# The value rows of a PEER expert layer, loaded by indirect transfers from GpSimd's queue instead of plain transfers from the SP queue

## The chip, the cores and the metric

The kernel runs on one core of one Trainium2 chip. Its engines are TensorE (PE for the multiplications, PEld for the weight loads that overlap them), VectorE (DVE), ScalarE (ACT), GpSimd (POOL) and SyncE (SP). Transfers between DRAM and the on-chip buffers are issued from the queue of an engine and carried out by the core's 16 DMA engines. The metric is device time in microseconds (us), lower is better.

## What is computed

One decoder layer on 256 tokens of width 1024: modulated norms, an input projection, two kinds of attention, their gated merge, and then a PEER feed-forward layer, in float32. Only the end of that last layer is touched by the change:

```python
def peer_ffn(h, w_pq, peer_keys, peer_u, peer_v):
    ...                      # routing: 128 experts of 16384 and a gate for each, per token
    u = jnp.take(peer_u, ec, axis=0)
    act = jax.nn.gelu(jnp.einsum('cd,ckd->ck', xc, u))
    vv = jnp.take(peer_v, ec, axis=0)
    return jnp.einsum('ck,ckd->cd', gc * act, vv)
```

`peer_v` has 16384 rows of 1024 floats, 64 MB in all. The kernel does not gather a token's 128 experts: it works out the activations of all 16384 experts for all tokens, multiplies them with gates that are zero for every expert that a token did not choose, and multiplies the result with the whole of `peer_v`. So every row of `peer_v` is read once, in an order that is known when the kernel is built.

## The kernel before, in words

The experts form a grid of 128 by 128. Expert number i * 128 + j stands in row i and column j, and the kernel takes one column j at a time: the 128 experts of a column lie on the 128 partitions. Two neighbouring columns make a pair, so there are 64 pairs.

The U side (`upair`, L551) works out the activations of a pair: 48 matmuls of 256 columns into `pus` or `pum`, then a gelu. For the first 58 pairs (columns below `J0` = 116) this is done early, beside the routing, and the result, 256 KB per pair, goes to DRAM (`act_spill`). The other 6 pairs, called direct here, are worked out in the V stage itself.

The V stage (from L740) is where the change lies. `order` (L747 to L752) mixes the 6 direct pairs with the 58 stored ones: two direct pairs first, then a direct one after each 12 or so stored ones. The loop at L778 takes the pairs in that order. For each pair it

- loads the stored activations `a` of the pair two places ahead from the SP queue (`act_of`, L758), into one of two buffers,
- multiplies `a` with the gates in place (`weighted`, L764, on DVE) and splits the product into a rounded part `wh` (ACT, L81) and the rest `wl` (DVE, L82); the end of `wl` frees the `a` buffer,
- loads the value rows of its two columns (`unit`, L784, which issues L91), 512 KB for each column: partition i gets row i * 128 + j, 4 KB, so the 128 rows of one load lie 512 KB apart in DRAM; each is split into `h_v` (ACT, L81) and `l_v` (DVE, L82), and the end of `l_v` frees the load's buffer `raw`,
- issues 24 matmuls of 512 columns into `acc` (`v_mm`, L85 to L87 through `mm3`).

The load's buffer has the tag `raw` and four places, which the U side's loads (`r_u`) and the V side's (`r_v`) share and take in turn; `hi` and `lo` have four places each as well. `a`, `wh` and `wl` have two. The order of the instructions on each engine is set when the kernel is built, by a scheduler that goes by priorities and modelled times; an engine then works through its list in order, and an instruction that waits holds up what is behind it on the same engine. GpSimd has no work in the kernel before but four small memsets at its start.

Before the V stage, the gate grid is built (`grid_mm`, L709, matmuls `pg` at L714) from buffers of the pool `onehot`, which are closed at L737, and their room is given to the pools of the V stage, `weights_in` and `weighted` (L741, L742). After it come the residual and the last norm.

Of the kernel before, what the change touches and what calls it, by code (L numbers as in the profile page):

```python
# [7 lines left out]
F32 = mybir.dt.float32  # L8
# [10 lines left out]
P = 128  # L19
# [4 lines left out]
EPS = 1e-6  # L24
# activations of the first J0 columns of experts are worked out while the routing goes on and kept in DRAM
J0 = 116
# steps of the routing, and batches of gates, to a pair of such columns
PACE_R = 2.5
PACE_G = 2.0
# the first norm's scales (even) and shifts (odd) that the tensor engine works out  # L30
ON_PE = (0, 1, 2, 3)
# [3 lines left out]
def kernel(  # L35
# [25 lines left out]

# [1 line left out]
    cpool = ctx.enter_context(tc.tile_pool(name="consts", bufs=1))  # L63
# [32 lines left out]
    def rsqrt(r, m, q, n=1):  # L96
        # 1 / sqrt(m) for n columns, halves m: first guess from the exponent, then Newton steps to float32's
        # accuracy
        nc.vector.tensor_scalar(r.bitcast(I32), m.bitcast(I32), 1, None, op0=OP.arith_shift_right)
        nc.vector.tensor_scalar(  # L100
            r.bitcast(I32), r.bitcast(I32), -1, 0x5F3759DF, op0=OP.mult, op1=OP.add
        )
        nc.vector.tensor_scalar(m, m, -0.5, None, op0=OP.mult)
        for _ in range(3):
            for i in range(n):
                c = slice(i, i + 1)
                nc.vector.scalar_tensor_tensor(q[:, c], r[:, c], r[:, c], m[:, c], op0=OP.mult, op1=OP.mult)
            for i in range(n):
                c = slice(i, i + 1)
                nc.vector.scalar_tensor_tensor(r[:, c], q[:, c], 1.5, r[:, c], op0=OP.add, op1=OP.mult)  # L110
# [10 lines left out]

# [1 line left out]
    es_a = ExitStack()  # L123
# [38 lines left out]
    def ada1(k):  # L162
        # scale and shift of row block k; some from the weights as they come on the tensor engine
        raw = spool.tile([P, 2, D], F32, tag="ada", bufs=3, name=f"ada1_{k}")
        nc.sync.dma_start(raw, w_ada[2 * k : 2 * k + 2].rearrange("k p d -> p k d"))
        got = []
        for i in range(2):
            t = 2 * k + i
            if t in ON_PE:
                row = pp.tile([1, P], F32, tag="pp", name=f"row_{t}")  # L170
                wk = raw[:, i].rearrange("p (k n) -> p k n", k=NC8)
                for j in range(NC8):
                    nc.tensor.matmul(row, cc[:, j : j + 1], wk[:, j], start=(j == 0), stop=(j == NC8 - 1))
                rs = spool.tile([1, P], F32, tag="rs", bufs=2, name=f"rs_{t}")
                nc.scalar.activation(rs, row, AF.Copy, scale=-1.0)
                cm = pm.tile([P, 1], F32, tag="mm", name=f"cm_{t}")
                nc.tensor.matmul(cm, rs, neg_one[0:1, 0:1], start=True, stop=True)
                got.append(cm)
            else:
                dots(raw[:, i : i + 1], t)  # L180
                got.append(mod[:, t : t + 1])
        g, b = gs[:, 0, k : k + 1], mod[:, 2 * k + 1 : 2 * k + 2]
        nc.vector.scalar_tensor_tensor(
            g, got[0], bcol1[:, k : k + 1], gcol[:, 0, k : k + 1], op0=OP.add, op1=OP.mult
        )
        nc.vector.tensor_add(b, got[1], bcol[:, 2 * k + 1 : 2 * k + 2])
        return g, b
# [10 lines left out]
    def rms(sq, name):  # L198
        # 1 / rms with tokens on partitions, then along them on all partitions
        ms = pz.tile([P, 2], F32, tag="z", name=f"ms_{name}")  # L200
        for tt in range(2):
            for i, s in enumerate(sq):
                nc.tensor.matmul(
                    ms[:, tt : tt + 1], s[:, P * tt : P * tt + P], mean_m,
                    start=(i == 0), stop=(i == len(sq) - 1),
                )
        rq = spool.tile([P, 3, 2], F32, name=f"rq_{name}")
        nc.vector.tensor_scalar(rq[:, 0], ms, EPS, None, op0=OP.add)
        rsqrt(rq[:, 1], rq[:, 0], rq[:, 2], 2)
        r = pm.tile([P, T], F32, tag="mm", name=f"r_{name}")  # L210
        for tt in range(2):
            dg = spool.tile([P, P], F32, tag="sq", bufs=2, name=f"dr_{name}{tt}")
            nc.vector.tensor_scalar(dg, ident, rq[:, 1, tt : tt + 1], -1.0, op0=OP.mult, op1=OP.mult)
            nc.tensor.matmul(r[:, P * tt : P * tt + P], neg_one, dg, start=True, stop=True)
        return r
# [19 lines left out]
    for k in range(NC8):  # L235
        nc.vector.tensor_mul(xr[:, k], x_sb[:, k], r1)
    # the first column blocks, for q and k, take each row block of h as its modulation arrives
    hh, hl = h_tiles("n1")
# [42 lines left out]

# [1 line left out]
    q_sb = apool.tile([P, 4, T], F32, name="q_sb")  # L283
# [26 lines left out]
    def roped(dst, ps, name):  # L310
        t1 = spool.tile([P, 2, T], F32, tag="att", bufs=6, name=f"t1_{name}")
        t2 = spool.tile([P, 2, T], F32, tag="att", bufs=6, name=f"t2_{name}")
        nc.vector.tensor_mul(t1, ps, rp[:, 0:1].to_broadcast([P, 2, T]))
        nc.vector.tensor_mul(t2, ps, rp[:, 1:2].to_broadcast([P, 2, T]))
        # rows of a pair of tiles: heads 0 2 1 3; two heads of 64 rows to each tile that is kept
        for i in range(2):
            nc.vector.tensor_sub(dst[:, i], t1[:, 0], t2[:, 1])
        for i, to, at in ((0, 32, 0), (0, 96, 64), (1, 0, 32), (1, 64, 96)):
            nc.vector.tensor_add(dst[to : to + 32, i], t2[at : at + 32, 0], t1[at : at + 32, 1])
# [23 lines left out]

# [1 line left out]
    o_hi = apool.tile([P, 6, T], F32R, name="o_hi")  # L345
# [48 lines left out]

# [1 line left out]
    def dilated(h, o):  # L396
# [81 lines left out]

# [1 line left out]
    m_hi = hpool.tile([P, NC8, T], F32R, tag="hh", name="m_hi")  # L480
# [65 lines left out]

# [1 line left out]
    es_s = ExitStack()  # L548
# [23 lines left out]

# [1 line left out]
    sel_pool = es_s.enter_context(tc.tile_pool(name="sel", bufs=1, side="right"))  # L574
    # per slot (head, rank): both halves of its expert's number, its gate in three parts
    selT = sel_pool.tile([P, 5, T], BF16, name="selT")
# [15 lines left out]
    for b in range(1, 8):  # L592
# [4 lines left out]
        nc.scalar.activation(qT[:, 2 * b : 2 * b + 2], ps, AF.Copy)  # L597
    # x1 with tokens on partitions, for the end
    for tt in range(2):
# [20 lines left out]
    for tt in range(2):  # L620
# [16 lines left out]
        nc.vector.tensor_copy(i_top, i_u)  # L637
        # pairs (a, b) of ranks with (a + 1) * (b + 1) > 16 have 16 pairs before them, so
        # a < 4 with every b and a >= 4 with b < 4 hold the 16 best, in the order of a * 16 + b
        cand = rpool.tile([P, 8, 112], F32, tag="cand", name=f"cand{tt}")  # L640
# [61 lines left out]

# [1 line left out]
    gpool = ctx.enter_context(tc.tile_pool(name="grid", bufs=1))  # L704
# [4 lines left out]
    def grid_mm(b, A, Bs):  # L709
        # a gate's parts add up to it without error  # L710
        ps = pg.tile([P, 4, P], F32, tag="g", name=f"pg{b}")
# [27 lines left out]

# [1 line left out]
    apl = ctx.enter_context(tc.tile_pool(name="weights_in", bufs=2))  # L741
    wpool = ctx.enter_context(tc.tile_pool(name="weighted", bufs=2))  # L742
    po = ctx.enter_context(tc.tile_pool(name="po", bufs=1, space=PSUM))
    acc = [po.tile([P, 512], F32, name=f"acc{i}") for i in range(4)]
    vv = v.rearrange("(i j) d -> j i d", j=NJ)
    direct, stored = list(range(J0, NJ, 2)), list(range(0, J0, 2))
    order = [direct.pop(0)]  # L747
    while direct or stored:
# [29 lines left out]
    for n, j in enumerate(order):  # L778
# [3 lines left out]
        if n + 2 < n_pairs:  # L782
            acts.append(act_of(order[n + 2]))
        vs = [unit(vv[j + s], f"v{j + s}", k=1) for s in range(2)]  # L784
        if n == n_pairs - 3:
# [25 lines left out]

# [1 line left out]
    # 1 / sqrt(sum / D + EPS) is sqrt(D) / sqrt(sum + D * EPS), and sqrt(D), a power of two, is in gfb  # L813
    st = wpool.tile([P, 2, 8], F32, tag="dg", name="st")
# [37 lines left out]
def _arrays(inputs):  # L852
# [10 lines left out]
    a["c"] = f["c"]  # L863
    # scale and shift of the first norm by turns, then gate 1, scale 2, shift 2, gate 2; all transposed but
    # for those that the tensor engine works out
    w = f["w_ada"][0]
# [64 lines left out]
```

## Time and profile before

| | us |
|---|---|
| two timed runs of the kernel before | 1109.73 and 1114.26, median 1111.99 |
| profiled execution, span from the first to the last instruction | 1112.9 |
| the V stage in it, first to last matmul into `acc` | 715.9 to 1103.6 |

The page gives the span of the profiled execution and no other time for it; that span lies 0.9 us above the median of the timed runs and within them. TensorE ran at its upper clock level in nearly all of the span (a granted share of 0.990 as a mean). Times in the rows are counted from the start of the span. A matmul's listed duration overlaps those of its neighbours, so the pace of TensorE is read from the distance between two starts.

### The profile page before, as it was taken

How to read it: one execution, taken by the hardware profiler on the slowest of the kernel's cores; microseconds unless marked ns; L12 is line 12 of the kernel's file. 1: busy time of each engine (PE TensorE's matmuls, PEld its weight loads, DVE VectorE, ACT ScalarE, POOL GpSimd, SP SyncE). 2: the span in 40 equal slices, each digit the busy share in tenths (PEclk: the TensorE clock that was granted, in tenths of full speed). 3: DMA queues.
4: the chain of work that ended last, by engine and by line, in shares of the span. 5: the costliest groups of instructions: out<-in, count | busy, mean ns of one | idle time of the engine just before them, and what ended most of it. 6: DMA issues, size and time to landing. Idle time of an engine off the chain costs nothing.

```text
span 1112.9 us, 19549 instructions
## 1 busy us (share of the span) xinstructions
PE 1077.8 (97%) x7671; PEld 984.2 (88%) x7674; DVE 833.5 (75%) x1539; ACT 557.8 (50%) x706; POOL 0.2 (0%) x4
## 2 busy tenths in 40 slices
PE   6899999999999999999999999999999999999986
PEld 4878988998999999999999999988887878888865
DVE  6777877686699889877877777677676767676675
ACT  4476344564465545554454544544444444445432
POOL 0000000000000000000000000000000000000000
PEclk9999999999999999999999999999999999999998
DMA  9954566453976765765555555576766667768751
GB/s 336 362 195 175 173 220 223 153 174 125 333 258 209 232 218 198 247 208 176 187 181 180 190 178 177 178 246 220 232 210 236 217 237 232 236 223 274 253 200 38
DMA packets 74206, 237.58 MB, mean 213 GB/s; under 512 B 8449, under 2 KB 8833, under 8 KB 73986
## 3 DMA queue, kind: packets, MB, share of 16 engines
q1 hardware_dynamic: 64898, 220.04, 58.7%
q10 hardware_dynamic: 9216, 16.29, 4.0%
q8 instruction: 60, 0.98, 0.4%
q14 instruction: 32, 0.26, 0.1%
HBM read 219.00 MB, written 17.30 MB: 212 GB/s over the span
## 4 chain that ended last, share of the span: by engine, by line
PE 60%; DMA 9%; DVE 8%; issue 3%; ACT 1%; DVEq 0%; SPq 0%; ACTq 0%
PE pus L85 9%; PE pus L86 8%; PE pus L87 8%; DMA a<-act_spill 8%; PE acc L87 6%; PE acc L86 6%; PE acc L85 6%; PE pg L714 4%; DVE wl L82 2%; DVE l_v L82 2%; PE p_pq L85 1%; PE p_pq L86 1%; PE p_pq L87 1%; DVE l_u L82 1%; DMA act_spill<-as 1%
## 5 line engine op out<-in xcount | busy, mean ns | idle before, releaser
L85 PE MATMUL pus<-hh_n,h_u 128*128 128x256 f32 x928 | 265.7, 286 | 0.0
L86 PE MATMUL pus<-hl_n,h_u 128*128 128x256 f32 x928 | 262.6, 283 | 0.0
L87 PE MATMUL pus<-hh_n,l_u 128*128 128x256 f32 x928 | 262.4, 283 | 0.0
L81 ACT ACTIVATE h_u<-r_u 128x1024 fp32r<-128x1024 f32 x128 | 135.5, 1060 | 180.9 <-PE pus L86 150.3
L87 PE MATMUL acc<-h_v,wl 128*128 128x512 f32 x512 | 201.3, 393 | 2.0 <-DVE wl L82 1.5
L86 PE MATMUL acc<-l_v,wh 128*128 128x512 f32 x512 | 200.9, 392 | 0.6 <-DVE l_v L82 0.6
L85 PE MATMUL acc<-h_v,wh 128*128 128x512 f32 x512 | 200.1, 391 | 0.0
L81 ACT ACTIVATE h_v<-r_v 128x1024 fp32r<-128x1024 f32 x128 | 135.0, 1056 | 119.1 <-PE acc L87 53.3
L82 DVE TENSOR_TENSOR l_u<-r_u,h_u 128x1024 fp32r<-128x1024 f32 x128 | 155.2, 1219 | 30.8 <-ACT h_u L81 30.5
L86 PEld LDWEIGHTS pus<-hl_n,h_u 128*128 128x128 f32 x928 | 178.0, 192 | 0.0
L87 PEld LDWEIGHTS pus<-hh_n,l_u 128*128 128x128 f32 x928 | 177.9, 192 | 0.0
L85 PEld LDWEIGHTS pus<-hh_n,h_u 128*128 128x128 f32 x928 | 177.8, 192 | 0.0
L82 DVE TENSOR_TENSOR l_v<-r_v,h_v 128x1024 fp32r<-128x1024 f32 x128 | 154.3, 1220 | 15.3 <-ACT h_v L81 15.1
L764 DVE TENSOR_TENSOR a<-a,G 128x512 f32<-128x512 f32 x64 | 70.3, 1099 | 99.0 <-DMA a<-act_spill 99.0
L87 PEld LDWEIGHTS acc<-h_v,wl 128*128 128x128 f32 x512 | 96.5, 189 | 26.1 <-DVE wl L82 6.3
L86 PEld LDWEIGHTS acc<-l_v,wh 128*128 128x128 f32 x512 | 96.7, 189 | 22.0 <-DVE l_v L82 2.1
L85 PEld LDWEIGHTS acc<-h_v,wh 128*128 128x128 f32 x512 | 96.6, 189 | 19.5
L730 DVE TENSOR_TENSOR B<-E,selT 128x768 bf16<-128x768 bf16 x128 | 68.1, 552 | 33.1 <-PE pg L714 33.1
L81 ACT ACTIVATE wh<-a 128x512 fp32r<-128x512 f32 x64 | 40.4, 631 | 78.3 <-PE acc L86 69.9
L151 DVE SCALAR_TENSOR_TENSOR junk<-ada,c_sb 128x1024 bf16<-128x1024 f32 x44 | 53.5, 1217 | 2.5 <-DMA ada<-in_w_ada_dram 2.2
L714 PE MATMUL pg<-B,A 128*128 128x128 bf16 x768 | 52.0, 222 | 0.1
L714 PEld LDWEIGHTS <-A 128*128 128x128 bf16 x768 | 46.9, 114 | 1.6
(319 smaller groups left out, 1837.9 us busy)
## 6 DMA issues: line engine op xcount, KB each, us to landing
r_u<-in_u_dram SPq DMA_DIRECT2D x128, 512.0 KB, 3.9
r_v<-in_v_dram SPq DMA_DIRECT2D x128, 512.0 KB, 4.4
ada<-in_w_ada_dram SPq DMA_DIRECT2D x20, 1024.0 KB, 7.3
act_spill<-as ACTq DMA_DIRECT2D x58, 256.0 KB, 2.5
a<-act_spill SPq DMA_DIRECT2D x58, 256.0 KB, 3.7
r_g<-in_w_in_dram SPq DMA_DIRECT2D x16, 512.0 KB, 3.6
r_pq<-in_w_pq_dram SPq DMA_DIRECT2D x16, 512.0 KB, 6.0
r_first<-in_w_in_dram SPq DMA_DIRECT2D x8, 512.0 KB, 7.4
```

Of the source, the lines that this page charges most:

```text
L81: nc.scalar.activation(hi, src, AF.Copy)
L82: last_split[:] = [nc.vector.tensor_sub(lo, src, hi.bitcast(F32))]
L85: nc.tensor.matmul(ps, lh, rh, start=start, stop=False)
L86: nc.tensor.matmul(ps, lh, rl, start=False, stop=False)
L87: nc.tensor.matmul(ps, ll, rh, start=False, stop=stop)
L151: nc.vector.scalar_tensor_tensor(junk, raw[:, k], 1.0, c_sb, op0=OP.mult, op1=OP.mult, accum_out=mod[:, t + k : t + k + 1])
L714: nc.tensor.matmul(ps[:, t], A[:, :, t], Bs[t // 2][:, x, :, t % 2], start=(x == 0), stop=(x == 2))
L730: nc.vector.tensor_tensor(B, E[:, None, :, 2 * q : 2 * q + 2].to_broadcast([P, 3, P, 2]), g, op=OP.mult)
L764: nc.vector.tensor_mul(a, a, G[:, :, j : j + 2].rearrange("p t s -> p s t"))
```

## The change

The value rows are no longer loaded by `unit` from the SP queue. A table of row numbers, `rows`, with i * 128 + j at partition i and column j, is made once by an `iota` on GpSimd, in the pool `weights_in`. For each column j GpSimd then issues an indirect transfer, which takes the 128 row numbers of column j and fetches those rows of `v`. The bytes, their place in `raw`, and the split are as before. The 128 loads of `r_v` leave the SP queue; the loads of `a`, of `r_u` and those at the end stay there. The rest of the diff removes comments.

```diff
@@ before: line 741, after: line 741 @@
     apl = ctx.enter_context(tc.tile_pool(name="weights_in", bufs=2))
     wpool = ctx.enter_context(tc.tile_pool(name="weighted", bufs=2))
     po = ctx.enter_context(tc.tile_pool(name="po", bufs=1, space=PSUM))
     acc = [po.tile([P, 512], F32, name=f"acc{i}") for i in range(4)]
-    vv = v.rearrange("(i j) d -> j i d", j=NJ)
     direct, stored = list(range(J0, NJ, 2)), list(range(0, J0, 2))
+    rows = apl.tile([P, NJ], I32, bufs=1, name="rows")
+    nc.gpsimd.iota(rows, pattern=[[1, NJ]], base=0, channel_multiplier=NJ)
+
+    def v_unit(j):
+        raw = stream.tile([P, D], F32, tag="raw", name=f"r_v{j}")
+        nc.gpsimd.indirect_dma_start(
+            out=raw, out_offset=None, in_=v, in_offset=bass.IndirectOffsetOnAxis(ap=rows[:, j : j + 1], axis=0)
+        )
+        hi, lo = [stream.tile([P, D], F32R, tag=t, name=f"{t[0]}_v{j}") for t in ("hi", "lo")]
+        split(hi, lo, raw)
+        return hi.rearrange("p (k n) -> p k n", k=1), lo.rearrange("p (k n) -> p k n", k=1)
+
...
-        vs = [unit(vv[j + s], f"v{j + s}", k=1) for s in range(2)]
+        vs = [v_unit(j + s) for s in range(2)]
```

## Rows read from the trace of the kernel before

**Rows 1.** Part 1 of the page: busy time, share and instructions of each engine.
```profile
PE 1077.8 (97%) x7671; PEld 984.2 (88%) x7674; DVE 833.5 (75%) x1539; ACT 557.8 (50%) x706; POOL 0.2 (0%) x4
```

**Rows 2.** Windows, the V stage: busy time and instructions of each engine, clock, DMA share.
```profile
core 0: us, PE busy (x) PEld busy (x) DVE busy (x) ACT busy (x) POOL busy (x), PEclk, DMA share, GB/s
715.00:1103.00 388.00, 380.60 (x1751) 314.41 (x1751) 268.32 (x281) 179.73 (x207) 0.00 (x0) 0.99 0.66 220
```

**Rows 3.** Tile `acc`, two of three matmul forms: ns min/median/max, first and last start.
```profile
L85 PE MATMUL acc<-h_v,wh x512: 387/389/628, 715.9 to 1102.8; 128*128 128x512 f32 x171
...
L87 PE MATMUL acc<-h_v,wl x512: 387/389/628, 716.4 to 1103.2; 128*128 128x512 f32 x171
```

**Rows 4.** Timeline of PE, one pair of the V stage: first and 25th matmul.
```profile
809.21 0.39 PE L87 MATMUL acc<-h_v,wl 128*128 128x512 f32 x1
...
814.65 0.39 PE L87 MATMUL acc<-h_v,wl 128*128 128x512 f32 x1
```

**Rows 5.** Windows of tile `pum` alone, around one direct pair: PE, PEld, ACT.
```profile
778.00:790.00 12.00, 5.92 (x48) 5.89 (x48) 0.58 (x1) 1.00 0.78 259
```

**Rows 6.** Waits of PE and PEld in the V stage: total us, times, longest.
```profile
PEld acc L87 <- DVE wl L82: 6.3, 14, 1.5
...
PE pgt L800 <- DVE dg L799: 4.8, 1, 4.8
...
PEld acc L86 <- DVE l_v L82: 2.1, 4, 0.7
```

**Rows 7.** Waits of the SP queue in the V stage.
```profile
SPq L91 <- DVE l_v L82: 184.5, 119, 6.2
SPq L758 <- DVE wl L82: 81.5, 53, 6.2
```

**Rows 8.** Waits of DVE and ACT in the V stage.
```profile
DVE a L764 <- DMA a<-act_spill: 99.0, 57, 3.5
ACT wh L81 <- PE acc L86: 69.9, 51, 1.9
...
ACT h_v L81 <- DMA r_v<-in_v_dram: 28.2, 17, 3.1
```

**Rows 9.** Tile `r_v`: its issues (ns, first and last start) and landings.
```profile
L91 SPq DMA_DIRECT2D r_v<-in_v_dram x128: 327/328/1292, 694.3 to 1078.8; - x128
...
DMA to landing us min/median/max: 3.4/4.4/6.3
```

**Rows 10.** Source line 758, the loads of `a`: landings.
```profile
DMA to landing us min/median/max: 2.5/3.7/6.3
```

**Rows 11.** Chain that ended last, two pairs: start, duration, what.
```profile
906.10 2.46 DMA a<-act_spill
...
909.68 1.23 DVE l_v L82
...
911.53 3.81 DMA a<-act_spill
...
916.45 0.70 DVE wl L82
917.16 2.47 DMA a<-act_spill
```

**Rows 12.** Timelines of SP, ACT and DVE in the same two pairs.
```profile
907.23 4.02 SPq L91 DMA_DIRECT2D r_v<-in_v_dram  x2
...
911.80 1.04 ACT L81 ACTIVATE h_v<-r_v 128x1024 fp32r<-128x1024 f32 x1
914.80 1.06 ACT L81 ACTIVATE h_v<-r_v 128x1024 fp32r<-128x1024 f32 x1 [1.95 <-DMA r_v<-in_v_dram]
...
917.05 1.22 DVE L82 TENSOR_TENSOR l_v<-r_v,h_v 128x1024 fp32r<-128x1024 f32 x1
...
920.74 1.21 DVE L82 TENSOR_TENSOR l_v<-r_v,h_v 128x1024 fp32r<-128x1024 f32 x1
```

**Rows 13.** Start of the V stage: chain (first row), then timelines of SP and ACT.
```profile
702.15 2.35 PE pg L714 x36
...
694.29 21.48 SPq L91 DMA_DIRECT2D r_v<-in_v_dram  x7
...
707.34 1.06 ACT L81 ACTIVATE h_v<-r_v 128x1024 fp32r<-128x1024 f32 x1 [2.21 <-PE pum L86]
710.22 1.06 ACT L81 ACTIVATE h_v<-r_v 128x1024 fp32r<-128x1024 f32 x1 [1.82 <-PE pum L86]
711.18 0.58 ACT L760 ACTIVATE a<-pum 128x512 f32<-128x512 f32 x1
```

## The prediction, made before the changed kernel was run

> **What bounds the kernel now.** I read the engines' busy times first. TensorE is busy for 97% of the span and POOL for 0.2 us [rows 1], so POOL has room, and the question is what the V stage waits for. A busy TensorE may still run below its pace, so I worked that out for the stage. One pair's 24 matmuls into `acc` take 814.65 - 809.21 = 5.44 us from start to start, or 0.2267 us each [rows 4]. A direct pair's 48 matmuls load weights for 5.89 us in a row, 0.123 us each [rows 5]. The stage has 1536 matmuls of the first kind (3 forms of 512 each [rows 3]) and four direct pairs whose matmuls fall inside it: 1536 x 0.2267 + 4 x 5.89 = 348.2 + 23.6 = 371.8 us. From the first matmul, at 715.9, to the end of the last, 1103.2 + 0.4 [rows 3], it took 387.7 us. So some 16 us are lost, 1.4% of the whole time: one wait of 4.8 us for `dg` near the end, 6.3 us for `wl`, 2.1 us for `l_v` [rows 6], and the rest at the stage's two ends. This is the first result: nothing that happens to the loads can give back more than 16 us. The 704 us before the gate grid's last matmuls hold no part of the change.
>
> Next, does the SP queue hold the loads back? It waits for `l_v` before an `r_v` and for `wl` before an `a`, 266 us together [rows 7]. Those are waits for a free buffer, not for a turn. In the rows, the load of `a` at 906.10 goes out when its buffer is free, and the load at 907.23 when `l_v` ends [rows 11, 12]. Taking `r_v` off SP therefore brings no load forward by itself.
>
> What does run close to TensorE's pace is a loop through `a`: the end of `wl` frees its buffer, the load lands, DVE multiplies it, splits, and frees the other buffer. Two turns of it take 917.16 - 906.10 = 11.06 us [rows 11] against 2 x 5.44 = 10.88 us of matmuls, and DVE waits 99.0 us in the stage for `a` [rows 8]. The loop holds landings of 2.46 and 3.81 us [rows 11], so the landing of `a` is the one DMA time that sets the pace, in the stretches where it does so.
>
> **The change, part by part.** *Removed from SP:* 128 issues of 0.33 us, 42 us of a queue that mostly waits [rows 9, 7]. Nothing else was late behind them: 0 us.
>
> *Added on POOL:* 128 indirect issues. The trace has no such instruction. From below, POOL may need no longer than SP's 0.33 us [rows 9]; from above, I take a POOL that is held until its transfer has landed, 4.4 us at the median [rows 9]. The nearest row is SP's issue of the same transfer. Software that has to read 128 numbers and build 128 addresses will be slower than that, so I take 1.1 us, still far nearer to that row than to the other. The Trainium skill ("DMA: Bandwidth & Descriptors", section "Latency and other measured facts") gives about 1 us to the first byte for a transfer issued by GpSimd and 0.6 us for one issued by SP. By that alone a load would land 0.4 us later, which the cover below hides as well as it hides 1.1 us; no row here shows a transfer from GpSimd.
>
> What covers 1.1 us? A load is issued when its buffer is free. The loads of rows 12 went out at 907.23 and, the second of the two, 4.02 - 0.33 us later, at 910.9. Their `h_v` began at 911.80 and 914.80, the second after a wait of 1.95 us for the data. Their `l_v` came only at 917.05 and 920.74, because DVE stood at `a`. From the end of `h_v` that is 4.2 and 4.9 us of slack. So even the load that ACT already waits for may be some 4 us later before DVE sees it. ACT waited for an `r_v` 17 times, 28.2 us [rows 8]; behind a late `h_v` on ACT stands the next `wh`, which itself waits 1.4 us on average for TensorE (69.9 / 51 [rows 8]). So 1.1 us later costs 0 in the steady stage. If the cover is gone, a pair loses what exceeds it, on 62 pairs. The rate fits too: 128 loads at 1.1 us are 141 us of POOL in a stage of 388 us.
>
> *The landing of `a`:* it stays on SP and no longer queues there behind an `r_v`. The `a` at 906.10, with no new `r_v` just ahead of it, landed in 2.46 us; the one at 911.53 came 0.6 us after an `r_v` and took 3.81 us [rows 11, 12]. After the change that `r_v` would leave POOL 1.1 us late and behind the `a`. Over the stage the landings of `a` run from 2.5 to 6.3 us, 3.7 at the median [rows 10], so there is room to either side. The loop could fall below TensorE's pace and give back the waits for `wl` and `l_v`, 8.4 us [rows 6]. But both queues use the same 16 DMA engines, which are 66% busy in the stage [rows 2], and a load that is sent from another queue may also interleave with an `a` that now runs ahead of it. From -8 to +8 us; I take 0.
>
> *The table and the start:* the room for `rows` comes from `onehot`, which the last `pg` matmuls use until 702.15 + 2.35 = 704.5 us [rows 13]. The `iota` (128 x 128 numbers; four POOL memsets take 0.05 us each [rows 1], and DVE's instruction on an `a`, four times as wide, at most 1.1 us, between the landing at 911.53 + 3.81 and the `wl` at 916.45 [rows 11]) is put at 0.3 us. The first load then leaves at 704.8 instead of 694.3, is handed over at 705.9, and lands 4.4 us later, at 710.3; the second lands at 711.4. In the kernel before, their splits began at 707.34 and 710.22 [rows 13]. The second split then ends at 712.5, and the gelu at 711.18, which stands behind it on ACT, is 1.3 us late, and with it the first weights and the first matmul into `acc`: +1.3 us. At POOL's lower end this is 0; at 4.4 us an issue the second load lands at 718.0, after which the stage starts 8 us late.
>
> *Queues passed:* the `r_u` of the direct pairs stay on SP and take their turn in `raw` between loads from POOL; an `r_u` that waits there for an `l_v` still holds up the `a` behind it, as before: 0. The loads at the end (`gb`, `x1`) only lose neighbours on SP: 0. The scheduler may place instructions otherwise when a load's queue is another; that can shift a wait such as the 4.8 us for `dg`, up or down, and I can't work out which.
>
> **Sum.** 1112.9 + 0 + 0 + 1.3 = 1114.2 us in terms of the profiled span, which lies 0.9 us over the median of the runs: 1113.3 us, rounded to 1113. About 2% (22 us) is what a measurement of this kernel can tell from no change, and this is well inside.
>
> **Rivals.** *1. POOL can't keep up.* If an indirect issue holds POOL for longer than 388 / 128 = 3.0 us, the issues set the pace from then on: 705 + 128 x 3.3 = 1127 us for the last issue, then the last landing, the split and the last matmuls and the norm. In the kernel before, 34 us follow the last issue at 1078.8 [rows 9], 5 of which are the wait for `dg`, so some 30: 1157 us at 3.3 us an issue. For it: the upper bound of 4.4 us lies above 3.0, and 128 row numbers are handled by a program. Against it: the transfer's size and rows are those of a transfer that SP issues in 0.33 us. At the full 4.4 us it would be 705 + 563 + 30 = 1298. Chance 0.18.
>
> *2. DVE and POOL get in each other's way.* All of DVE's work in the loop (`a` times gates, `wl`, `l_v`) reads two operands from the same memory that holds the row numbers. If an issue on POOL holds DVE for its 1.1 us, twice a pair, DVE's wait for `a` (99.0 / 57 = 1.7 us [rows 8]) takes up part of it. At best 2.2 - 1.7 = 0.5 us is added to each of the 58 stored pairs, at worst one whole hold of 1.1 us: 29 to 64 us, or 1142 to 1177, and I put it at 1160. It decides from a hold of 0.85 us, half of the 1.7. For it: DVE is 268 us busy and 99 us waiting of 388 [rows 2, 8], so it has nothing else to give. Against it: no row shows POOL at work beside DVE. Chance 0.10. The Trainium skill ("SBUF — State Buffer", section "Who interferes with whom") has this rule: a DVE instruction with two inputs from the SBUF contends with a GpSimd instruction that reads the SBUF, and whichever comes first holds the shared port for its whole length. It also holds that writing descriptors needs the other half of the port, so the rule bites only if the row numbers are read that way.
>
> *3. The loop through `a` is relieved and the order at the end comes out better.* The 8.4 us for `wl` and `l_v` and the 4.8 us for `dg` go: 1113 - 13 = 1100 us. For it: the 2.46 us landing with no load just ahead. Against it: the shared DMA engines. Chance 0.10. A gain of more than 22 us would need more than the stage loses.
>
> *4. The indirect form isn't what it says,* and the transfer goes out as a plain one: the rows are in a fixed order, so this would change nothing and gives 1112; it is within the likeliest case.
>
> **How the numbers follow.** Likeliest, 0.62: the loads are later and hidden, 1113, itself from 1104 to 1125. Rival 1 has 0.18 (1140 and up), rival 2 0.10 (1142 to 1177), rival 3 0.10 (about 1100). The range runs from 1100, which leaves half of rival 3 out, to 1160, which takes in the lower half of rivals 1 and 2. Slower by over 2%: 0.27 of these two. Faster by over 2%: 0.02. Within: 0.71.
>
> **What would show it.** Right: POOL's issues near 1 us, the wait of ACT for `r_v` longer than 28 us, PE's and PEld's waits in the V stage still under 20 us, the first matmul into `acc` near 717, the last load issued near 1080. Wrong: POOL busy without gaps (rival 1), DVE instructions longer than 1.22 us (rival 2), or TensorE waiting for `l_v` in most pairs, which would mean that the loads' lateness is beyond the 4 us that I read as slack.

## The result and the profile after

The changed kernel took 1122.09 us (1120.79 and 1123.38), the kernel before 1111.99 us: a ratio of 1.008, with a 95% interval of 1.0051 to 1.011. It is some 10 us slower, well inside the forecast range, near its middle case in size and not in cause, as the experiments show. The span of its profiled execution is 1121.6 us, 8.7 us longer than before.

The page's busy times (part 1), as [rows 1]:

```profile
PE 1080.0 (96%) x7671; PEld 986.4 (88%) x7674; DVE 832.6 (74%) x1539; ACT 557.7 (50%) x706; POOL 140.4 (13%) x133
```

POOL now has 128 issues to make. The tile view of `r_v` gives their cost and landings, as [rows 9] (durations in ns minimum/median/maximum; then first and last start in us):

```profile
L751 POOL DMA_INDIRECT r_v<-in_v_dram,rows x128: 932/1012/1794, 708.1 to 1087.1; - x128
L82 DVE TENSOR_TENSOR l_v<-r_v,h_v x128: 1209/1219/1234, 713.6 to 1101.7; 128x1024 fp32r<-128x1024 f32 x128
...
DMA to landing us min/median/max: 4.1/4.8/9.1
```

The line of the loads of `a` gives theirs, as [rows 10]:

```profile
DMA to landing us min/median/max: 2.4/2.7/6.8
```

Value rows land in 4.8 us at the median, where plain ones took 4.4, and `a` in 2.7, where it took 3.7. Both are counted from the start of the issue, so POOL's own time is inside the 4.8. This view can date 51 of the 58 loads of `a`; by the packet records of the trace, which have all of them, the mean went from 3.6 to 3.2 us. So the value loads came later and most `a` quicker. DVE's `l_v` is as long as before.

The waits in the V stage, engine by engine, as [rows 6 to 8] (us in all, times, longest):

```profile
PEld acc L87 <- DVE wl L82: 6.3, 11, 2.4
PEld acc L86 <- DVE l_v L82: 5.8, 3, 4.0
...
SPq L769 <- DVE wl L82: 322.4, 56, 26.4
...
DVE a L775 <- DMA a<-act_spill: 100.8, 54, 5.7
...
ACT h_v L81 <- DMA r_v<-in_v_dram,rows: 78.6, 39, 3.8
...
POOL r_v L751 <- DVE l_v L82: 218.8, 106, 7.0
```

ACT now waits 78.6 us for value rows instead of 28.2. TensorE feels little of it; what grew is a few waits for `l_v`, the longest 4.0 us.

To see where the 8.7 us lie I took the start of each pair's first matmul from the trace. The part before the V stage, whose code is unchanged, ended 2.3 us later in this execution. From there to the first matmul into `acc` it took 1.1 us longer, pairs 0 to 12 took 1.6 longer, pairs 12 to 50 2.2 *shorter*, pairs 50 to 61 6.2 longer (67.8 against 61.6), and the last two pairs and the norm 0.2 shorter. So the steady middle gained, and the loss lies at the ends, most of it among the last twelve pairs. The chain that ended last shows the largest piece there (start and duration in us):

```profile
1046.08 1.22 DVE l_v L82
1047.30 0.61 DVE wl L82
...
1047.93 6.75 DMA a<-act_spill
```

An `a` that left when `wl` had ended landed 6.75 us later, and that pair took 11.3 us instead of 5.4. POOL's timeline has two value loads that were issued just ahead of it:

```profile
1045.20 1.79 POOL L751 DMA_INDIRECT r_v<-in_v_dram,rows  x1 [2.07 <-issue]
1047.57 1.14 POOL L751 DMA_INDIRECT r_v<-in_v_dram,rows  x1 [0.58 <-DVE l_v L82]
```

TensorE's clock explains little of the loss: its granted share is 0.987 as a mean, against 0.990 before. In the V stage it stayed at 1.00 up to 1053 us and fell to 0.84 from there to 1064, after TensorE had stood still behind this `a`.

One thing is not seen in any sum of waits. In the instruction lists of the two kernels TensorE's order is the same, but on DVE the scheduler placed some 30 of the 128 `l_v` otherwise. In the kernel before, DVE's timeline alternates:

```profile
908.65 1.12 DVE L764 TENSOR_TENSOR a<-a,G 128x512 f32<-128x512 f32 x1 [1.44 <-DMA a<-act_spill]
909.68 1.23 DVE L82 TENSOR_TENSOR l_v<-r_v,h_v 128x1024 fp32r<-128x1024 f32 x1
910.81 0.69 DVE L82 TENSOR_TENSOR wl<-a,wh 128x512 fp32r<-128x512 f32 x1
911.41 2.36 DVE L82 TENSOR_TENSOR l_v<-r_v,h_v 128x1024 fp32r<-128x1024 f32 x2
915.43 1.10 DVE L764 TENSOR_TENSOR a<-a,G 128x512 f32<-128x512 f32 x1 [1.66 <-DMA a<-act_spill]
916.45 0.69 DVE L82 TENSOR_TENSOR wl<-a,wh 128x512 fp32r<-128x512 f32 x1
```

In one pair an `l_v` stands between `a`*G and `wl`; in the next it has been done earlier and `wl` follows at once. In the changed kernel most pairs have it in between, 47 of them against 29. Its timeline of DVE:

```profile
959.02 1.09 DVE L775 TENSOR_TENSOR a<-a,G 128x512 f32<-128x512 f32 x1 [1.90 <-DMA a<-act_spill]
960.04 1.22 DVE L82 TENSOR_TENSOR l_v<-r_v,h_v 128x1024 fp32r<-128x1024 f32 x1
961.17 0.68 DVE L82 TENSOR_TENSOR wl<-a,wh 128x512 fp32r<-128x512 f32 x1
961.77 1.21 DVE L82 TENSOR_TENSOR l_v<-r_v,h_v 128x1024 fp32r<-128x1024 f32 x1
964.48 1.10 DVE L775 TENSOR_TENSOR a<-a,G 128x512 f32<-128x512 f32 x1 [1.49 <-DMA a<-act_spill]
```

And its timeline of POOL over the same time, with one issue beside DVE's work and one while DVE waits:

```profile
961.52 1.14 POOL L751 DMA_INDIRECT r_v<-in_v_dram,rows  x1 [3.19 <-DVE l_v L82]
963.26 0.94 POOL L751 DMA_INDIRECT r_v<-in_v_dram,rows  x1 [0.59 <-DVE l_v L82]
```

This matters because the loop through `a` runs over DVE: `wl` ends, the next `a` loads, `a`*G, whatever DVE has before `wl`, `wl`. From these starts, one turn is the landing + 1.03 (`a`*G) + 0.72 (`wl`), some 1.8 us over the landing with the handing over, and with an `l_v` inside (1.13 more) 2.9 us over it. TensorE needs 5.44 us a pair. So `a` may land in 3.65 us where no `l_v` is inside and in 2.5 us where one is; in the order of before, with one every second pair, in 3.1 us as a mean. The change took 0.55 us a pair from this room by the order, and gave 1.0 us back by the median landing (0.4 by the mean). That is a first reading; the experiments test it.

### The profile page after: what moved, and what is told of

It reads as the page before. It is cut to its first block, busy times and chain, and to the rows that moved or that the text cites. A ratio compares the mean times of both kernels' runs of the same rounds, so it can differ in the third digit from the quotient of the medians.

```text
span 1121.6 us, 19575 instructions
## 1 busy us (share of the span) xinstructions
PE 1080.0 (96%) x7671; PEld 986.4 (88%) x7674; DVE 832.6 (74%) x1539; ACT 557.7 (50%) x706; POOL 140.4 (13%) x133
## 4 chain that ended last, share of the span: by engine, by line
PE 67%; DVE 7%; DMA 5%; issue 1%; ACT 1%; SPq 0%; POOL 0%; DVEq 0%; ACTq 0%; POOLq 0%
PE acc L87 9%; PE acc L86 9%; PE acc L85 9%; PE pus L85 8%; PE pus L86 8%; PE pus L87 8%; PE pg L714 4%; DMA a<-act_spill 2%; PE p_pq L85 1%; DMA act_spill<-as 1%; PE p_pq L86 1%; PE p_pq L87 1%; DVE l_u L82 1%; DVE l_v L82 1%; DMA gb<-in_g_final_dram 1%
## 5 line engine op out<-in xcount | busy, mean ns | idle before, releaser
L81 ACT ACTIVATE h_v<-r_v 128x1024 fp32r<-128x1024 f32 x128 | 134.9, 1055 | 141.2 <-DMA r_v<-in_v_dram,rows 78.6
L751 POOL DMA_INDIRECT r_v<-in_v_dram,rows x128 | 140.0, 1094 | 240.9 <-DVE l_v L82 218.8
```

The costliest lines, as they stand in the source:

```text
L81: nc.scalar.activation(hi, src, AF.Copy)
L751: nc.gpsimd.indirect_dma_start(out=raw, out_offset=None, in_=v, in_offset=bass.IndirectOffsetOnAxis(ap=rows[:, j : j + 1], axis=0))
```

## The experiments

All ran in rounds beside the kernel before, which gave 1114.85, 1112.98, 1114.17 and 1113.40 us in the four sets. Ratios are to it.

**The two ends.** First I held the table and the order of the last loads responsible (theory A, against B: every value load leaves POOL a little late, and the stage pays for that in small pieces). *Table early*: `rows` lives in another pool and is made at the kernel's start.

```diff
+    rows = cpool.tile([P, NJ], I32, name="rows")
+    nc.gpsimd.iota(rows, pattern=[[1, NJ]], base=0, channel_multiplier=NJ)
...
-    rows = apl.tile([P, NJ], I32, bufs=1, name="rows")
-    nc.gpsimd.iota(rows, pattern=[[1, NJ]], base=0, channel_multiplier=NJ)
```

> The changed kernel with the row numbers made at the very start, in a room of their own, so that the first load from POOL no longer waits for the gate grid's buffers. The order of the instructions on PE, DVE and ACT is that of the changed kernel. Theory A (the time is lost at the two ends of the V stage: at its start behind the table of row numbers, at its end behind the 1 MB load of x1 that the scheduler now puts ahead of an a and of gb on SP): the first matmul into acc comes 2 to 3 us sooner against the last pg matmul, and the total falls by 2 to 3 us from 1122. Theory B (every load is late by POOL's 1.09 us and the slower landing, and the stage pays for that in small pieces): under 1 us.

Measured: 1123.75 us, 1.0084 (1.0053 to 1.0114). The first loads left at 693.5 instead of 708.1, and nothing of it reached the end.

*`gb` first*: the 1 MB load of `x1`, which the scheduler had moved ahead of `gb` on SP, is held behind it.

```diff
-            nc.sync.dma_start(gfb, g_final.to_broadcast([P, D]))
+            got_g = nc.sync.dma_start(gfb, g_final.to_broadcast([P, D]))
...
-            nc.sync.dma_start(x1, x1_spill.rearrange("a p d -> p a d"))
+            with tc.issue_after(got_g.ins):
+                nc.sync.dma_start(x1, x1_spill.rearrange("a p d -> p a d"))
```

> The changed kernel with the load of x1 held back until the load of gb is issued, as it stood in the kernel before. Theory A: ACT's instruction on gb no longer waits until 1030, no wait of TensorE near 1053 and no lower clock after it, 1114 to 1117 us. Theory B: no change from 1122 beyond 1 us.

Measured: 1124.0 us, 1.0098 (1.0066 to 1.0129). *Both edits together:*

> Both edits, the early table and gb ahead of x1. Theory A: 1111 to 1115 us, that is no difference from the kernel before that can be told. Theory B: still 1119 us or more.

Measured: 1123.01 us, 1.0071 (1.0046 to 1.0096). Theory A falls; theory B's expectations were met here.

**The same queue without the indirect form.** Plain transfers, issued by POOL; no table.

```diff
-        nc.gpsimd.indirect_dma_start(
-            out=raw, out_offset=None, in_=v, in_offset=bass.IndirectOffsetOnAxis(ap=rows[:, j : j + 1], axis=0)
-        )
+        nc.gpsimd.dma_start(raw, vv[j])
```

> The changed kernel with plain transfers from POOL's queue in place of the indirect ones, and no table. Orders on PE, DVE and ACT as in the changed kernel. Theory A: the form of the transfer is not what costs; the start gains 2 to 3 us because no table is waited for, the end loses what it lost, so 1119 to 1121 us. Theory B in the form that reading 128 row numbers is what costs: POOL's issue well under 1.09 us and a time back near 1112.

Measured: 1188.01 us, 1.0663 (1.0633 to 1.0693), outside both expectations. TensorE, DVE and ACT have the order of the changed kernel here, so taking the indirect form *away* costs 66 us. Its tile view of `r_v` has the issues:

```profile
L750 POOL DMA_DIRECT2D r_v<-in_v_dram x128: 527/527/662, 693.8 to 1150.5; - x128
```

Its line of the loads of `a` has their landings:

```profile
DMA to landing us min/median/max: 2.5/4.4/7.2
```

A plain issue holds POOL half as long, the value loads leave sooner, and `a` now shares the DMA engines with them: 4.4 + 2.9 = 7.3 us a turn. In the settled stretches (below) the pairs take 7.29 us.

**Order and transfer taken apart.** The order of `a`*G, `wl` and `l_v` on DVE is pinned by edges that carry no wait; nothing else is edited. Into the changed kernel goes the order of before, into the kernel before that of the changed one, and into the plain-from-POOL variant that of before. With M for `a`*G, W for `wl`, l for an `l_v` and the number of the pair, a stretch of before's order is `M6 l5.0 W5 l5.1 l6.0 M7 W6 l6.1`, and the changed kernel's is `M6 l5.0 W5 l5.1 M7 l6.0 W6 l6.1`.

```diff
+    def behind(late, early):
+        tc.add_manual_dep(
+            late, early.name, mybir.DependencyInfo(mybir.DependencyClass.NoSync, mybir.DependencyReason.DATA),
+            reason="order",
+        )
...
+    for early, late in zip(dve, dve[1:]):
+        behind(late, early)
```

The changed kernel with the order of before:

> The changed kernel, with the V stage's instructions on DVE (a*G, wl, l_v) held in the order of the kernel before. There every second pair has an l_v ahead of the a*G; in the changed kernel nearly every pair has that l_v between a*G and wl, so that it stands in the loop of `a` (wl end, load of a, a*G 1.03, l_v 1.13, wl 0.72). Theory D (the cost is this order, which the scheduler chose anew; a landing of `a` may take 2.5 us in a loop with the l_v and 3.65 us without, against TensorE's 5.44 us a pair): with a landing of 2.7 us the mean loop falls from 5.6 to 5.0 us, the late pairs 50 to 61 take some 62 us again instead of 68, total 1113 to 1117. Theory B' (the loads from POOL land later, and that is what costs): no change, 1122 within 3.

Measured: 1153.9 us, 1.0353 (1.0313 to 1.0393). Not 9 us faster but 32 slower: theory D, that the order of before is simply the better one, falls in this form, and B' ("no change") with it. Its waits of DVE and ACT in the V stage:

```profile
DVE a L776 <- DMA a<-act_spill: 133.2, 52, 6.5
...
ACT h_v L81 <- DMA r_v<-in_v_dram,rows: 120.7, 53, 4.3
```

Three of the issues in its timeline of POOL:

```profile
917.76 1.15 POOL L751 DMA_INDIRECT r_v<-in_v_dram,rows  x1 [4.04 <-DVE l_v L82]
919.50 1.68 POOL L751 DMA_INDIRECT r_v<-in_v_dram,rows  x1 [0.59 <-DVE l_v L82]
921.48 1.73 POOL L751 DMA_INDIRECT r_v<-in_v_dram,rows  x1 [0.30 <-issue]
```

In this order three `l_v` come close together in every second pair, so three value loads (1.5 MB) leave POOL one after the other. The view dates only 7 of the 58 loads of `a` in this run, with a median of 2.7 us; the packet records have all of them, and there the landings go by turns. The `a` that leaves with the first of the three value loads is ahead of them and lands in 2.7 us (median); the next falls on them and takes 5.4. Over all 58 the median is 3.8. Beside the three issues above, the `a` issued at 918.12 landed in 2.7 us and the one issued at 923.02 in 5.9, and DVE's timeline has the waits for these two:

```profile
921.29 1.10 DVE L776 TENSOR_TENSOR a<-a,G 128x512 f32<-128x512 f32 x1 [0.92 <-DMA a<-act_spill]
929.25 1.05 DVE L776 TENSOR_TENSOR a<-a,G 128x512 f32<-128x512 f32 x1 [5.12 <-DMA a<-act_spill]
```

With 1.8 and 2.9 us of DVE's time, two turns make 2.7 + 5.4 + 4.7 = 12.8 us; two settled pairs (below) took 13.4.

The kernel before with the order of the changed one:

> The kernel before (plain loads from SP), with the V stage's instructions on DVE held in the order of the changed kernel. Theory D: the loop becomes landing + 2.9 us in nearly every pair; with before's median landing of 3.7 us that is 6.6 us against 5.44, on some 45 of the 58 stored pairs that change order (about half of them) or are already so: +25 to +65 us, 1137 to 1177. Theory B': the order costs nothing, 1112 within 4.

Measured: 1146.64 us, 1.031 (1.028 to 1.0341), within theory D's range: the order alone, with plain loads on SP, costs 34 us. (The scheduler also moved some small matmuls on `dg`, and the last two pairs and the norm became 4.4 us shorter, so the other pairs lost more than 34.) Its chain shows the loop at work:

```profile
887.84 1.22 DVE l_v L82
889.06 0.62 DVE wl L82
...
889.69 3.59 DMA a<-act_spill
...
894.36 1.22 DVE l_v L82
895.58 0.61 DVE wl L82
...
896.20 3.94 DMA a<-act_spill
```

From load to load it takes 6.51 us here, and `a` lands in 3.8 us at the median of the stage.

The plain-from-POOL variant with the order of before:

> The variant with plain loads from POOL (1188 us), with DVE held in the order of the kernel before. Theory D: half of the pairs lose 1.13 us from the loop, 7.3 to 6.75 us a pair, some 32 us: 1150 to 1165. If instead the competition of the value loads with `a` on the DMA engines is all of the 66 us: 1188 within 5.

Measured: 1137.59 us, 1.0213 (1.0187 to 1.0239): some 50 of its 76 us over the kernel before are gone by order alone, more than theory D had worked out (1150 to 1165).

**A third buffer for `a`** in the changed kernel, which lets an `a` load a pair earlier (`ones` and `dg` lie in a part of `gb` that is filled later, to make room).

```diff
-        a = apl.tile([P, 2, T], F32, tag="a", name=f"a{j}")
+        a = apl.tile([P, 2, T], F32, tag="a", bufs=3, name=f"a{j}")
...
-            ones = wpool.tile([P, P], F32, name="ones")
+            ones = gtb[:, 512 : 512 + P]
...
-                    dg = wpool.tile([P, P], F32, tag="dg", name=f"dg{q}{k}")
+                    dg = gtb[:, 640 + P * (k % 3) : 768 + P * (k % 3)]
```

> The changed kernel with three buffers for `a` in place of two (room for it from placing `ones` and `dg` in a part of gb that is not yet in use). The load of an `a` then has a whole pair, 5.44 us, more of cover. Theory D, and any theory in which the loop through `a` is what costs: the loop is gone, 1110 to 1117. Theory B' (the value loads are late): 1122 within 3.

Measured: 1117.88 us (1112.63 to 1125.95), 1.0054 (1.0018 to 1.0091). Between the theories, its interval meets that of the changed kernel, and the scheduler moved a few instructions on TensorE and DVE as well: no verdict on the total. Its pairs 50 to 61 took 70.5 us, more than the 67.8 of the changed kernel, and its last two pairs and the norm 28.0 instead of 35.2. So a third buffer did not regain what the late pairs lose.

**An order in which the loop is short.** If the loop is what counts, the order to take is `a`*G, `wl`, `l_v`, `l_v`: nothing stands in the loop, and each `a` leaves before the two `l_v` that let value loads go. The same edges, in each of the three kinds of transfer:

```diff
+    for n in range(4, n_pairs - 1):
+        if max(order[n : n + 3]) < J0:
+            behind(v_rest[n], w_rest[n])
+            behind(w_rest[n], gated[n + 1])
```

Indirect, from POOL:

> The changed kernel, with DVE held to the order a*G, wl, l_v, l_v in the stored pairs, so that no l_v stands in the loop of `a`, and each load of `a` leaves before the two l_v that let the value loads go. Theory E (the loop is the landing of `a` plus what DVE's order puts into it, and the landing grows with the value loads beside it): loop 2.6 + 1.8 = 4.4 us against TensorE's 5.44, a microsecond of slack a pair, so the late pairs are regained: 1110 to 1117; the later start (1 to 3 us) stays. Rival (lateness of the indirect loads is the cost, whatever the order): 1120 to 1126.

Measured: 1135.18 us, 1.0181 (1.0152 to 1.0211), slower than both expectations.

Plain, from SP:

> The kernel before (plain loads from SP) with the same order a*G, wl, l_v, l_v. Theory E: `a` leaves SP ahead of the value loads and lands in 2.5 to 3 us, loop 4.3 to 4.8 us: at TensorE's pace, 1106 to 1113. Rival (two l_v in a row bunch the value loads, so that they miss their turn): slower than before, 1118 to 1130.

Measured: 1103.17 us (1101.47 to 1104.42), 0.9901 (0.988 to 0.9923): faster than both kernels, and than theory E's range. DVE waits 60.0 us for `a` instead of 99.0, and TensorE's weight loads hardly wait any more:

```profile
DVE a L765 <- DMA a<-act_spill: 60.0, 57, 3.7
...
ACT h_v L81 <- DMA r_v<-in_v_dram: 8.0, 4, 2.7
...
PEld acc L87 <- DVE wl L82: 1.4, 1, 1.4
PEld acc L86 <- DVE l_v L82: 0.6, 2, 0.4
```

Of the gain, 3.6 us lie in pairs 12 to 50, 1.4 in 50 to 61, and 7.5 in the last two pairs, where the wait for `dg` [rows 6] shrank to 0.4 us (one of the small matmuls on `dg` also moved by a place).

Plain, from POOL:

> Plain value loads from POOL (1188 us with the changed kernel's order, 1138 with that of before) with the order a*G, wl, l_v, l_v. Theory E: a plain load from POOL has its first packets 0.9 us after its issue, so `a` has some 2 us of the DMA engines for itself and lands in some 3 us; loop 4.8 us: 1110 to 1122, with which the 75 us were order and not the queue. Rival (a second queue beside SP's costs by sharing the DMA engines): 1135 or more.

Measured: 1109.83 us, 0.9962 (0.9942 to 0.9982), just below theory E's range. So what this variant lost, 66 us against the changed kernel and 76 against the kernel before, goes away with another order on the same queue. But theory E does not explain the indirect case. The chain of that kernel shows what is special there:

```profile
899.94 0.69 DVE wl L82
...
900.65 2.53 DMA a<-act_spill
...
904.28 0.69 DVE wl L82
...
904.98 6.27 DMA a<-act_spill
...
912.39 0.69 DVE wl L82
...
913.09 2.59 DMA a<-act_spill
```

The landings of `a` alternate. One pair is over in 4.3 us, its successor's `a` then leaves while the last pair's value loads are under way (POOL's issues are at 902.51 and 904.01, and at 906.85 and 908.35 for the next pair), and takes 6.3: together 12.4 us for two pairs instead of 10.88.

**Lateness alone.** The indirect issue holds POOL for 1.18 us at the median in that kernel, a plain one for 0.53, and its first packets, by the packet records of the trace, come 2.3 us after its start, against 1.3. To see whether that lateness is the cost I made the plain loads later: POOL first writes a part of the buffer. All engines have the same order in the three kernels.

```diff
+        nc.gpsimd.memset(raw[:, 0:640], 0.0)
         nc.gpsimd.dma_start(raw, vv[j])
```

> Plain value loads from POOL in the order a*G, wl, l_v, l_v (1109.8 us), with one thing added: ahead of each load POOL writes 640 of its buffer's 1024 columns, which the load then overwrites. So each load waits for its buffer as before, then for some 0.6 to 0.9 us of this writing, and goes out later by that. The indirect form with the same order on every engine took 1135.2 us; its issue is held 1.18 us in place of 0.53 and its first packets come 2.3 us after the issue's start in place of 1.3. Theory L (what the indirect form costs in this order is that its loads start about a microsecond later): 1122 to 1140. Rival (the form itself, by its descriptors or its row numbers, and not the lateness): 1105 to 1116.

The tile view gives the delay that was added:

```profile
L750 POOL MEMSET r_v<- x128: 629/637/656, 695.4 to 1078.2; 128x640 f32 x128
L751 POOL DMA_DIRECT2D r_v<-in_v_dram x128: 530/530/664, 696.3 to 1079.2; - x128
```

With 0.30 us from its end to the issue that is 0.94 us. Measured: 1112.4 us, 0.9988 (0.9965 to 1.001): 2.6 us, and the intervals meet, as the rival had it. `a` lands in 3.5 us instead of 2.9, which a loop of 1.8 us over the landing still bears. Not all of the 0.94 us reached the loads. Counted from the issue of the pair's `a`, the pair's two value loads have their first packets at some 3.0 and 3.9 us in the plain variant, 3.6 and 5.1 with the delay, and 4.2 and 5.7 in the indirect one (their issues, medians over some 40 pairs, and behind them the 1.3, 1.5 and 2.3 us from an issue to its first packet, medians too). So theory L falls for the first 0.6 to 1.2 us of lateness; the last 0.6 us, with which the second load begins only after the next `a`, 5.44 us on, was not tried.

What the runs say together, in us (the settled pair is the mean distance between two pairs over 18 of them, six ahead of the matmuls of each of the last three direct pairs, by when the lead that a direct pair gives is used up; worked out from the starts of the matmuls; the landing is the view's median, and the two rows marked "by turns" are those whose loads of `a` alternate, the first of them with the median of all packet records):

```
transfer of the value rows, order on DVE        time     settled pair   landing of `a`
plain, SP       before's                      1112.0        5.55            3.7
indirect, POOL  changed kernel's              1122.1        5.47            2.7
indirect, POOL  before's                      1153.9        6.68            3.8, by turns 2.7 and 5.4
plain, SP       changed kernel's              1146.6        6.77            3.8
plain, POOL     changed kernel's              1188.0        7.29            4.4
plain, POOL     before's                      1137.6        6.02            4.3
plain, SP       a*G, wl, l_v, l_v             1103.2        5.44            3.0
plain, POOL     a*G, wl, l_v, l_v             1109.8        5.44            2.9
plain, POOL, 0.94 us later, the same          1112.4        5.44            3.5
indirect, POOL  a*G, wl, l_v, l_v             1135.2        6.12            3.9, by turns 2.6 and 5.6
```

## Why the prediction came out as it did

The change is two changes, and they nearly cancel (the times come from different sets, whose kernel before agrees within 3 us). The order alone costs 1146.6 - 1113.0 = 34 us; the indirect transfers, in that new order, gain 1146.6 - 1122.1 = 24.5 us. The other way round, the transfers alone cost 1153.9 - 1113.0 = 41 us and the new order then gains 32. Either way some 10 us are left. The forecast of 1113 was near by luck: two effects of 24 to 41 us, neither of which it had, nearly cancelled.

- *The bound.* TensorE sets the pace: right. The 16 us that could be given back stand: the best run gave back 11, and its settled pairs are at 5.44 us. How much could be *lost* was not bounded by this, and the same loads lost 76 us in one run.
- *128 issues off SP, 0 us:* right. With all of them on SP the stage reaches TensorE's pace.
- *POOL at 1.1 us an issue:* right, 1.094 us as a mean (140.0 us for 128). Rival 1 falls: the last issue begins at 1087.1, and POOL mostly waits for `l_v` (218.8 us).
- *Landing of a value load.* The Trainium skill ("DMA: Bandwidth & Descriptors", "Latency and other measured facts") made it 0.4 us later by its first bytes. The medians, 4.8 and 4.4, differ by as much, but they are counted from the start of the issue, with POOL's 1.1 us and SP's 0.33 inside, so this does not bear the 0.4 out. The first packets do show POOL's loads later: 2.2 us after the start of an issue that holds POOL for 1.0 (medians). In all a value load landed some 0.4 us later after its issue began, less than the 1.1 that I had asked the slack to cover.
- *"1.1 us later costs 0 in the steady stage", from 4 us of slack:* this step failed. The slack was read from rows in before's order, and in just that order the indirect loads cost 41 us. I counted only until DVE reached its own `l_v`, and not what the loads do to the `a` beside them: from POOL's queue they fall on every second `a`, which then takes 5.4 us. Plain loads from POOL in this order cost 25 us (1137.6 - 1113.0), so more than half of the 41 goes with the other queue and the rest with the indirect form; how much of that rest is its lateness, no run in this order tells. The settled pairs of the changed kernel are not slower because the scheduler took another order with the later loads.
- *"From -8 to +8 us; I take 0" for the landing of `a`:* both of its directions came true, the quicker `a` in the new order (3.8 with plain loads, 2.7 with the indirect ones, where the transfers gained 24.5 us) and the `a` that meets loads from another queue in the old one (5.4 us every second time, where they cost 41). The bounds were far too narrow, since they were made from waits that TensorE showed, not from what one microsecond in the loop does over 58 pairs.
- *"The scheduler may place instructions otherwise":* named, and given the size of a wait for `dg`. It was the other 34 us.
- *The start, +1.3 us:* the `iota` took 0.23 us (I put 0.3) but began at 706.90, after the last copy into G had made room (timeline of POOL):

```profile
706.90 0.23 POOL L747 IOTA rows<- 128x128 int32 x1 [706.46 <-ACT G L717]
708.11 1.08 POOL L751 DMA_INDIRECT r_v<-in_v_dram,rows  x1 [0.98 <-DMA act_spill<-as]
```

  The first matmul came 1.1 us later, near the forecast, and the next pairs lost 1.6. The early table shows that regaining this does not help the total.
- *Rival 2, DVE held by POOL:* falls. `l_v` takes 1.219 us as before. The Trainium skill ("SBUF — State Buffer", "Who interferes with whom") says that whichever comes first holds the shared port. No run shows DVE lengthened; POOL is. In the changed kernel's trace 57 of the 128 issues ran with DVE idle and took 0.936 us as a mean, and 57 ran with DVE busy throughout and took 1.229; a plain issue took 0.53 us either way.
- *Rival 3, the `a` loop relieved, 1100:* its parts, 8.4 us for `wl` and `l_v` and 4.8 for `dg`, are what the run at 1103.2 us gave back, but that needed another order on DVE and not this transfer. Rival 4 falls: the plain transfer from POOL behaves quite otherwise.
- *The tells:* ACT's wait for `r_v` beyond 28 us, POOL's issues near 1 us, the wait of PEld for `acc` under 20 us and the first matmul near 717 (719.2, of which 2.3 lay ahead of the stage) all came true, and none of them shows why; DVE's order in the timeline would have. The last load was issued at 1087.1, not near 1080.

What stays open. Why pairs 50 to 61 lose 6 us in the changed kernel. The pair of 11.3 us has its `a` of 6.75 us, which met value loads from POOL; the 1.5 MB for `gb` and `x1` had landed by 1030.3, 17 us earlier, and reordering them did not help. What set the value loads to meet this `a` is not known. With 5.47 us a pair the loop has little room to recover, but the run with a third buffer, which should give that room, lost more in these pairs, so this is not shown to be the reason. And why the indirect form costs 25 us in the order `a`*G, `wl`, `l_v`, `l_v`, where 0.94 us of delay cost 2.6: the alternation is shown, what starts it is not. That the scheduler reordered DVE because it models a load from POOL as later is a guess.

## What to carry to other kernels

When a load changes its queue, compare the order of the compute instructions around it before comparing durations: here reordered `l_v` weighed 34 us and the new transfer 24.5 the other way. Find the loop that runs through a double buffer, count what the in-order engine does inside it, and take the room as TensorE's time for a turn less that; a large load that may overlap the small load of this loop is then the thing to place. Putting the end of the loop (`wl`) ahead of work that only frees the next large loads was worth 1% here, the wait for `dg` at the end included, with the transfers left as they were.

## What was not expected of the hardware

- A plain 512 KB transfer holds POOL for 0.53 us and an indirect one for 0.94 us with DVE idle and 1.23 us with DVE busy; DVE does not slow down for it.
- First packets came 2.2 us after the start of an indirect issue (median in the changed kernel) and 1.3 to 1.5 us after that of a plain one from POOL.
- A 256 KB load of `a` landed in 2.5 to 2.8 us when other transfers took 1% of the DMA engines' time between its first and its last packet, and in 5.7 us at the median when they took 71% of it (20 and 26 loads of the run at 1135.2 us, by its packet records).
